# A hybrid encoder layer on one core: w_down's columns taken back and forth, and partial sums put into the banks of the last products

## The chip, the core and the metric

The kernel runs on one core of a Trainium2 chip, and the metric is the device time of one execution in microseconds. TensorE (PE) multiplies matrices and writes to PSUM, eight banks of 128 x 512 fp32; VectorE (DVE) and ScalarE (ACT) read and write both PSUM and the on-chip memory SBUF. Transfers between DRAM and SBUF are asked for on two queues: SyncE's (SP), and GpSimd's (POOL), where a transfer can also add to what stands in DRAM (an accumulating DMA). Both queues are served by the same 16 DMA engines. Each engine and each queue works through its instructions in the order in which they were written; semaphores hold an instruction until what it needs is there.

## What is computed

One layer over 512 tokens of width 2048: RMSNorm, one projection, local attention in one half of the heads and gated linear attention in the other, `w_out`, a residual sum, and then the part that this change touches:

```python
    h = rmsnorm(x, ffn_norm_w[l])
    x = x + (jax.nn.silu(h @ w_gate[l]) * (h @ w_up[l])) @ w_down[l]

return rmsnorm(x, final_norm_w)
```

`w_gate` and `w_up` are 2048 x 5632 and `w_down` is 5632 x 2048. All is fp32. The kernel gets fp32 accuracy from three products of a faster type: every operand is split into a rounded part `hi` and a rest `lo`, and hi*hi, hi*lo and lo*hi are summed in PSUM.

## The kernel before

All engine code is written out by hand in one order. There is no scheduler: each Python call appends one instruction to its engine's queue, and the framework adds the semaphores. SBUF is handed out in slots: `s2` has 70 of 128 x 512, `s4` has 16 of 128 x 1024, `ps` the eight PSUM banks. A slot that was given back goes to the end of its list, and its next user waits until the last one is through.

**`Blocks`** (lines 1119 to 1176) multiplies with weights in 2 x 2 blocks with seven products instead of eight. One step takes one weight block of 512 KB. `load` asks for it on SP, with at most `most` blocks held; `sums` makes four sums on VectorE (L1155 to L1157); `split` makes hi on ScalarE (L1168) and lo on VectorE (L1173). Then `products` issues 42 matmuls of 256 columns. `run` writes for step i: load, split of step i, sums of i+1 and i+2, split of i+1, then the products of step i. So VectorE's list is a step or two ahead of TensorE's.

**`Feed`** is the gate and up projections. Its first five sums are made earlier, during `w_out` (`before_out`, with `most` up to 5, as half-size operations into `s2` slots). `run_urgent` takes one piece of the pending side work each time it is called; at the start that work is the last operands of the feed-forward input (L1033, L1036, ScalarE's L1047).

**`w_down`** has 44 row blocks of 128. Blocks 0 to 3 are multiplied directly in four early jobs, whose results are added to the residual kept in DRAM, `xd`. Blocks 4 to 35, as pairs q = 2 to 17, go through `Down` with the seven products. Blocks 36 to 39 follow in four jobs, one for each block of 512 columns (`later_first`, called the later jobs here), and blocks 40 to 43 in `finish`, token block by token block, with the final norm.

`Down` takes the pairs in three chunks (6, 5 and 5 pairs), and in each chunk the four column blocks c = 0 to 3, and in each of these the chunk's pairs: 64 steps. The operands of a chunk's pairs stay in SBUF over its four columns and are made for the next chunk during the fourth (`make`). Seven PSUM banks hold the seven products of one (chunk, column). At the last pair of each, `evac` copies each bank to SBUF (ScalarE, L1474 and L1476), and a DMA carries it to `md` in DRAM: a plain store on SP in the first chunk (L1481), an accumulating one on POOL afterwards (L1479). Four banks are evacuated at once and three (`late`) before the next step's products.

In the last chunk `ahead` loads, at the second pair of each column, the residual `x1` of the column from `xd` (L1459, four DMAs on SP), and for column 3 the seven sums from `md` as well (L1463). When a column is done, `combine` fetches its seven sums from `md` (L1497, on POOL), makes the four output blocks of them with seven operations (L1503 add, L1504 subtract) and adds them, scaled by `rstd2`, to `x1` (L1517, four operations). It runs piece by piece through `run_urgent`. For column 3 the last banks are added to `m` straight from PSUM (L1469).

The later jobs run through `run_job`: four halves of 12 matmuls of 512 columns (L302 to L304); the stream `st` loads their weights on SP (L183) and splits them (L198 on ScalarE, L199 on VectorE) with a lead of three halves or more; `g_load` and `g_split` (L1299 to L1303) do the same for the gated activations. At a job's end `residual` (L1322) adds each bank, scaled, to `x1`.

Of the kernel before, what the change touches and what calls it, by code (L numbers as in the profile page):

```python
# [117 lines left out]
def layer(nc, tc, x, attn_norm_w, w_in, rel_table, gw_f, gb_f, gw_b, gb_b, gla_norm_w, w_out,  # L118
# [7 lines left out]
    with tc.manual_schedule(), \  # L126
# [124 lines left out]
        class Job:  # L251
            drop = None
            between = None
            tail = None

# [11 lines left out]
        def run_job(j):  # L267
# [4 lines left out]
            banks = [ps.get() for _ in range(4)]  # L272
            per = len(j.kts) // j.n
            for i in range(j.n):
# [9 lines left out]
                for b in range(4):  # L284
                    if j.between:
                        j.between(i, b)
                    for s_, k in enumerate(ks):
# [9 lines left out]
                        else:  # L297
# [4 lines left out]
                            mm(o, xh.t[:, c], wh.t[:, w], start=first, stop=False)  # L302
                            mm(o, xh.t[:, c], wl.t[:, w], start=False, stop=False)  # L303
                            mm(o, xl.t[:, c], wh.t[:, w], start=False, stop=last)  # L304
# [874 lines left out]
        class Feed(Blocks):  # L1179
# [80 lines left out]
            def run(self):  # L1260
                banks = {}
                for i, (u, q) in enumerate(self.seq):
                    if u not in banks:
                        banks[u] = [ps.get() for _ in range(4)]
                    self.most = 3
# [4 lines left out]
                    self.split(i + 1)  # L1270
                    self.products(i, banks[u])
# [4 lines left out]
                    for _ in range(3 if i < 8 else 1):  # L1276
                        run_urgent()
# [76 lines left out]
        class Down(Blocks):  # L1354

            def __init__(self, chunks):
                self.chunks = chunks
                self.begin([(ch, c, q) for ch in range(len(chunks)) for c in range(4) for q in chunks[ch]], 1, 256)  # L1360
                self.x = {}
                self.making = self.operands()
                self.late = []

# [59 lines left out]
            def products(self, i):  # L1424
# [4 lines left out]
                first, last = q == self.chunks[ch][0], q == self.chunks[ch][-1]  # L1429
# [5 lines left out]
                for n, ((wh, wl), x) in enumerate(prods):  # L1435
# [16 lines left out]
                if c == 3:  # L1452
                    put(*self.x.pop(q)["slots"])

            def ahead(self, c):

                x1[c] = [s2.get() for _ in range(4)]
                for t in range(4):
                    sp.dma_start(out=x1[c][t].t, in_=xd[4 * c + t])  # L1459
                if c == 3:  # L1460
                    self.m = [s2.get(F32, [P, 2, 256]) for _ in range(7)]
                    for n in range(7):
                        sp.dma_start(out=self.m[n].t.rearrange("p s c -> p (s c)"), in_=md[7 * c + n])  # L1463

            def evac(self, ch, c, n, bank):

                if ch == len(self.chunks) - 1 and c == 3:
                    m = self.m[n].t.rearrange("p s c -> p (s c)")
# [15 lines left out]
            def evac_late(self):  # L1484
                for e in self.late:
                    self.evac(*e)
                if self.late and self.late[0][0] == len(self.chunks) - 1:
                    urgent.append(self.combine(self.late[0][1]))
                self.late = []

            def combine(self, c):
                if c == 3:
                    m = self.m
                else:
                    m = [s2.get(F32, [P, 2, 256]) for _ in range(7)]
                    for n in range(7):
                        pool.dma_start(out=m[n].t.rearrange("p s c -> p (s c)"), in_=md[7 * c + n])  # L1497
                    for _ in range(4):
                        yield
                M = [None] + [x_.t for x_ in m]  # L1500
                y = [s4.get(F32, [P, 2, 512]) for _ in range(2)]
                lo, up = slice(0, 256), slice(256, 512)
                add = lambda o, x_, y_: dve.tensor_tensor(o, x_, y_, op=OP.add)  # L1503
                sub = lambda o, x_, y_: dve.tensor_tensor(o, x_, y_, op=OP.subtract)  # L1504
                add(y[0].t[:, :, up], M[2], M[1])
                sub(M[3], M[1], M[3])
                yield
                sub(M[5], M[5], M[3])
                add(M[3], M[4], M[3])
                yield  # L1510
                sub(y[0].t[:, :, lo], M[5], M[7])
                add(y[1].t[:, :, up], M[6], M[3])
                yield
                sub(y[1].t[:, :, lo], M[5], M[4])
                put(*m)
                for t in range(4):
                    dve.scalar_tensor_tensor(x1[c][t].t, y[t // 2].t[:, t % 2], rstd2[:, t:t + 1], x1[c][t].t,  # L1517
                                             op0=OP.mult, op1=OP.add)
                    if t % 2:
                        yield  # L1520
                put(*y)

            def run(self):
                for i, (ch, c, q) in enumerate(self.seq):
# [6 lines left out]
                    self.evac_late()  # L1531
# [5 lines left out]
                    if c == 3 or i % 3:  # L1537
                        self.make(1)
                    for _ in range(2 if ch == len(self.chunks) - 1 and i % 2 else 1):
                        run_urgent()  # L1540
                    if ch == len(self.chunks) - 1 and c == 3:
# [179 lines left out]
```

## Time and profile before

| what | value |
|---|---|
| runs shown | 2231.3, 2232.7, 2233.52 us, median 2232.7 |
| the profiled execution | 2230.92 us, of which the profile's span is 2229.0 |
| TensorE matmul busy | 2206.4 us, 99% of the span |
| VectorE, ScalarE, GpSimd busy | 1632.0, 998.5, 108.1 us |
| `Feed` | about 862 to 1753 us |
| `Down`: chunk 0, 1, 2 | from 1796.9, 1917.8, 2018.6 us |
| last column of `Down` ends | about 2123 us |
| later jobs, then `finish` | about 2126 to 2176 us, to the end |

A row of groups in the profile gives the line, the engine, the operation, the tiles written and read (their numbers left out), the shapes and the count, then busy time, mean duration, and the idle time of the engine just before it with what ended it. A row of waits gives: who waited for whom, us in total, times, longest. A row of the table by stage gives, from:to, the length, then for TensorE's matmuls, its weight loads, VectorE, ScalarE and GpSimd the busy us and the count, then the granted clock of TensorE, the share of the 16 DMA engines that were busy (1 is all of them; small errors let it pass 1), and GB/s. In the views of DMA, q1 is SP's queue and q0 POOL's: packets, MB, share of the engines. A matmul is shown longer than the distance to the next one, as matmuls overlap.

### The profile page before, as it was taken

Reading aid. Unit: us, or ns where it says so; the run is one execution under the profiler, and the core shown is the slowest. Engines: PE = TensorE matmul, PEld = TensorE weight load, DVE = VectorE, ACT = ScalarE, POOL = GpSimd, SP = SyncE. Lnnn points to the kernel's source line nnn. Section 1 sums busy time; section 2 is a strip of 40 time slices with the busy share of each in tenths; the row PEclk is TensorE's granted clock in tenths of the full one; section 3 lists DMA queues with packets and bytes.
Section 4 is the critical chain, followed back from the end, with each engine's and each line's share of the span. In section 5 each row is a group of like instructions: output and inputs, shape, how many; then the busy total and the mean of one; then the engine's idle time right before and its main releaser. Section 6 shows DMA issues by size and latency. Waiting matters only on the chain.

```text
span 2229.0 us, 37056 instructions
## 1 busy us (share of the span) xinstructions
PE 2206.4 (99%) x14842; PEld 2039.6 (91%) x14842; DVE 1632.0 (73%) x2748; ACT 998.5 (45%) x1644; POOL 108.1 (5%) x163
## 2 busy tenths in 40 slices
PE   9999999999999999999999999999999999999988
PEld 7888888888888888999999999999999999999967
DVE  4366665644454447988888888888888788887985
ACT  6244454444453345434444344434443565555442
POOL 0000000000000100000000000000000110122300
PEclk9999999999999999999999999999999999999999
DMA  6525625231314432333333333333333865688962
GB/s 206 168 76 155 177 77 140 85 116 55 104 60 148 142 133 67 114 119 119 114 123 118 115 126 115 123 116 114 124 114 114 258 179 190 178 200 224 288 219 76
DMA packets 212201, 305.93 MB, mean 137 GB/s; under 512 B 15229, under 2 KB 133421, under 8 KB 212030
## 3 DMA queue, kind: packets, MB, share of 16 engines
q1 hardware_dynamic: 194366, 258.87, 36.4%
q0 software_dynamic: 17344, 44.18, 8.2%
q8 instruction: 116, 1.90, 0.3%
q10 hardware_dynamic: 320, 0.53, 0.1%
q14 instruction: 55, 0.45, 0.1%
HBM read 246.58 MB, written 44.37 MB: 131 GB/s over the span
## 4 chain that ended last, share of the span: by engine, by line
PE 94%; DVE 3%; DMA 2%; SPq 0%; issue 0%; ACT 0%; POOL 0%; DVEq 0%
PE ps L1216 13%; PE ps L1215 13%; PE ps L1214 13%; PE ps L303 6%; PE ps L304 6%; PE ps L302 6%; PE ps L296 5%; PE ps L294 5%; PE ps L295 5%; PE ps L1443 4%; PE ps L1444 4%; PE ps L1442 4%; PE ps L530 1%; DMA a<-md 1%; PE ps L870 1%; PE ps L539 1%
## 5 line engine op out<-in xcount | busy, mean ns | idle before, releaser
L1216 PE MATMUL ps<-a,b 128*128 128x256 f32 x2464 | 698.9, 284 | 1.8 <-DVE b L1173 1.8
L1214 PE MATMUL ps<-a,b 128*128 128x256 f32 x2464 | 698.9, 284 | 0.0
L1215 PE MATMUL ps<-a,b 128*128 128x256 f32 x2464 | 698.7, 284 | 0.0
L1168 ACT CAST b<-b 128x1024 fp32r<-128x1024 f32 (+1 forms) x475 | 439.9, 941 | 537.6 <-DVE b L1173 311.0
L1173 DVE TENSOR_TENSOR b<-b,b 128x1024 fp32r<-128x1024 f32 (+1 forms) x475 | 503.0, 1087 | 116.5 <-PE ps L1215 60.9
L1216 PEld LDWEIGHTS ps<-a,b 128*128 128x128 f32 x2464 | 474.0, 192 | 2.0 <-DVE b L1173 2.0
L1214 PEld LDWEIGHTS ps<-a,b 128*128 128x128 f32 x2464 | 474.0, 192 | 0.0
L1215 PEld LDWEIGHTS ps<-a,b 128*128 128x128 f32 x2464 | 473.9, 192 | 0.0
L199 DVE TENSOR_TENSOR a<-b,a 128x512 fp32r<-128x512 f32 x292 | 194.7, 686 | 142.5 <-ACT a L198 131.4
L1443 PE MATMUL ps<-b,a 128*128 128x256 f32 x896 | 254.5, 284 | 2.6 <-DVE b L1173 2.6
L1444 PE MATMUL ps<-b,a 128*128 128x256 f32 x896 | 254.1, 284 | 0.0
L1442 PE MATMUL ps<-b,a 128*128 128x256 f32 x896 | 254.0, 284 | 0.0
L198 ACT CAST a<-b 128x512 fp32r<-128x512 f32 x292 | 170.7, 618 | 42.9 <-DMA b<-in_w_in_dram 12.8
L303 PE MATMUL ps<-a,a 128*128 128x512 f32 x464 | 181.7, 392 | 4.6 <-DVE a L199 4.6
L302 PE MATMUL ps<-a,a 128*128 128x512 f32 x464 | 183.2, 395 | 2.8 <-ACT a L198 2.8
L304 PE MATMUL ps<-a,a 128*128 128x512 f32 x464 | 181.1, 390 | 0.0
L1443 PEld LDWEIGHTS ps<-b,a 128*128 128x128 f32 x896 | 172.3, 192 | 3.5 <-DVE b L1173 3.5
L1442 PEld LDWEIGHTS ps<-b,a 128*128 128x128 f32 x896 | 172.4, 192 | 0.0
L1444 PEld LDWEIGHTS ps<-b,a 128*128 128x128 f32 x896 | 172.3, 192 | 0.0
L1155 DVE TENSOR_TENSOR b<-b 128x512 f32<-128x512 f32 x235 | 160.8, 684 | 11.6 <-DMA b<-in_w_down_dram 11.6
L294 PE MATMUL ps<-a,a 128*128 128x512 f32 x416 | 167.0, 401 | 0.4 <-ACT a L198 0.4
L296 PE MATMUL ps<-a,a 128*128 128x512 f32 x416 | 162.9, 392 | 0.2
(243 smaller groups left out, 3072.0 us busy)
## 6 DMA issues: line engine op xcount, KB each, us to landing
b<-in_w_gate_dram SPq DMA_DIRECT2D x88, 512.0 KB, 3.5
b<-in_w_up_dram SPq DMA_DIRECT2D x88, 512.0 KB, 3.8
b<-in_w_down_dram SPq DMA_DIRECT2D x88, 512.0 KB, 6.1
b<-in_w_in_dram SPq DMA_DIRECT2D x48, 512.0 KB, 3.9
b<-in_w_in_dram SPq DMA_DIRECT2D x92, 256.0 KB, 4.2
b<-in_w_out_dram SPq DMA_DIRECT2D x32, 512.0 KB, 5.9
md<-a POOLq DMA_DIRECT2D x49, 256.0 KB, 8.4
a<-a SPq DMA_DIRECT2D x96, 128.0 KB, 2.3
```

The costliest lines, as they stand in the source:

```text
L294: mm(o, wh.t[:, c], xh.t, start=first, stop=False)
L302: mm(o, xh.t[:, c], wh.t[:, w], start=first, stop=False)
L303: mm(o, xh.t[:, c], wl.t[:, w], start=False, stop=False)
L304: mm(o, xl.t[:, c], wh.t[:, w], start=False, stop=last)
L1168: act.copy(o, src)
L1173: dve.tensor_tensor(o, src, h, op=OP.subtract)
L1214: mm(o, wh, xh, start=head, stop=False, skip_group_check=True)
L1215: mm(o, wh, xl, start=False, stop=False, skip_group_check=True)
L1216: mm(o, wl, xh, start=False, stop=end, skip_group_check=True)
L1442: mm(o, xh[:, t], wh, start=first and h == 0, stop=False, skip_group_check=True)
L1443: mm(o, xh[:, t], wl, start=False, stop=False, skip_group_check=True)
L1444: mm(o, xl[:, t], wh, start=False, stop=last, skip_group_check=True)
```

## The change

1. `Down` takes the columns of chunk 1 in the order 3, 2, 1, 0. So chunk 0's column 3 and chunk 1's column 3 follow each other, and the seven banks are not evacuated between; likewise column 0 from chunk 1 to chunk 2.
2. The combining no longer touches `x1`. It writes its result into the `md` tiles in SBUF, two operations a step, from four steps after the fetch. Column 3's `md` tiles are fetched on SP during column 2.
3. `seed` copies the combined blocks into four PSUM banks (ScalarE, eight copies of half a bank), and the later job of that column starts with its matmuls adding to these banks. One `residual` then adds all to `x1`. Column 0's seeds are copied during the last step of `Down`, the other columns' at the third half of the job before.
4. `x1` is loaded only in the later jobs, at the second half of each.
5. The first weights of the later jobs are asked for one step earlier, and a second load is allowed in the step after.
6. In `Feed`, five loads may be held in the first two steps and one more set of sums is made in each of them in the half-size form; `run_urgent` is called twice a step, not three times, in steps 2 to 7.

```diff
-            banks = [ps.get() for _ in range(4)]
+            banks = j.banks or [ps.get() for _ in range(4)]
...
+                            on = bool(j.banks)
+                            mm(o, xh.t[:, c], wh.t[:, w], start=first and not on, stop=False, skip_group_check=on)
...
-                    self.most = 3
+                    self.most = 5 if i < 2 else 3
...
+                    if i < 2:
+                        self.sums(self.n_sums, halves=True)
...
-                    for _ in range(3 if i < 8 else 1):
+                    for _ in range(3 if i < 2 else 2 if i < 8 else 1):
...
+                cols = lambda ch: range(3, -1, -1) if ch % 2 else range(4)
+                self.begin([(ch, c, q) for ch in range(len(chunks)) for c in cols(ch) for q in chunks[ch]], 1, 256)
...
+                third = 0 if ch % 2 else 3
+                first = q == self.chunks[ch][0] and (ch == 0 or c != 3 - third)
+                last = q == self.chunks[ch][-1] and (ch == self.end or c != third)
...
                             self.evac(ch, c, n, self.banks[n])
+                            if ch == self.end and c == 3:
+                                self.seed(0, n)
...
+            def fetch(self, c, ns, queue):
+
+                self.m.setdefault(c, {})
+                for n in ns:
+                    m = self.m[c][n] = s2.get(F32, [P, 2, 256])
+                    queue.dma_start(out=m.t.rearrange("p s c -> p (s c)"), in_=md[7 * c + n])
...
-                if ch:
+                if (c, n) in self.stored:
                     pool.dma_start(out=md[7 * c + n], in_=y.t, accum_op=OP.add)
                 else:
                     sp.dma_start(out=md[7 * c + n], in_=y.t)
+                    self.stored.add((c, n))
...
+            def evac_late(self, i):
+                late, self.late = self.late, []
+                for e in late:
                     self.evac(*e)
+                if late and late[0][0] == self.end:
+                    c = late[0][1]
+                    if c < 3:
+                        self.fetch(c, range(7), pool)
+                        i += 4
                     for n in range(7):
+                        self.ops.append((i, c, n))
+
+            def combine(self, i, n):
+
+                while n and self.ops and self.ops[0][0] <= i:
+                    _, c, k = self.ops.popleft()
+                    n -= 1
+                    m = self.m[c]
...
+                    dve.tensor_tensor(m[o].t, m[x_].t, m[y_].t, op=op)
...
+            def seed(self, c, t):
...
+                for h in range(2):
+                    act.copy(b.t[:, h * 256:(h + 1) * 256], self.y[c][t // 2][h].t[:, t % 2])
...
-                    if ch == len(self.chunks) - 1 and q == self.chunks[ch][1]:
-                        self.ahead(c)
...
+                    if ch == self.end:
                         n = self.chunks[ch].index(q)
+                        self.combine(i, 2)
+                        if c == 2 and n:
+                            self.fetch(3, range(2 * n - 2, min(2 * n, 7)), sp)
+                        if c == 3:
+                            if n == 0:
+                                g_load(LAST // 2 - 2)
+                            if n == 1:
+                                st.until, st.limit = None, 1
+                                st.load()
+                            if n == 2:
+                                g_split(LAST // 2 - 2)
+                                g_load(LAST // 2 - 1)
+                                st.limit = 2
+                                st.load()
...
-                run_urgent()
+                dn.combine(len(dn.seq), 2 if c else 1)
+                if i == 1:
+                    x1[c] = [s2.get() for _ in range(4)]
+                    for t in range(4):
+                        sp.dma_start(out=x1[c][t].t, in_=xd[4 * c + t])
+                if i == 2 and c < 3:
+                    for t in range(4):
+                        dn.seed(c + 1, t)
```

More of the change, by code (lines that the diff above doesn't have):

```diff
@@ L254, in layer @@
             tail = None
+            banks = None
         def job(kind, pieces, kts, acts, evac, rate=0.0, before=None, start=None, limit=None):
@@ L1359, in __init__ @@
                 self.chunks = chunks
-                self.begin([(ch, c, q) for ch in range(len(chunks)) for c in range(4) for q in chunks[ch]], 1, 256)
+                self.end = len(chunks) - 1
+                cols = lambda ch: range(3, -1, -1) if ch % 2 else range(4)
+                self.begin([(ch, c, q) for ch in range(len(chunks)) for c in cols(ch) for q in chunks[ch]], 1, 256)
                 self.x = {}
@@ L1363, in __init__ @@
                 self.late = []
+                self.stored = set()
+                self.m, self.y = {}, {}
+                self.ops = deque()
             def source(self, ch, c, q):
@@ L1451, in products @@
                     put(hi, lo)
-                if c == 3:
+                if c == third:
                     put(*self.x.pop(q)["slots"])
[L1455 to L1463, printed above, removed]
+            def fetch(self, c, ns, queue):
[3 more added lines that the diff above has]
+                    queue.dma_start(out=m.t.rearrange("p s c -> p (s c)"), in_=md[7 * c + n])
             def evac(self, ch, c, n, bank):
-                if ch == len(self.chunks) - 1 and c == 3:
-                    m = self.m[n].t.rearrange("p s c -> p (s c)")
+                if ch == self.end and c == 3:
+                    m = self.m[c][n].t.rearrange("p s c -> p (s c)")
                     dve.tensor_tensor(m, m, bank.t, op=OP.subtract if n == 4 else OP.add)
@@ L1491, in combine @@
[L1491 to L1495, printed above, removed]
-                    for n in range(7):
[L1497 to L1521, printed above, removed]
```

48 lines of the change are left out of this document (23 added, 25 removed).

## The prediction

> **What bounds the kernel now.** I read the busy shares, TensorE's waits, a table by stage, and then, stage by stage, what VectorE and the two DMA queues did before each wait.
>
> ```profile
> PE 2206.4 (99%) x14842; PEld 2039.6 (91%) x14842; DVE 1632.0 (73%) x2748; ACT 998.5 (45%) x1644; POOL 108.1 (5%) x163
> ...
> PE ps L303 <- DVE a L199: 4.6, 6, 1.4
> PE ps L302 <- ACT a L198: 2.8, 1, 2.8
> PE ps L1443 <- DVE b L1173: 2.6, 3, 1.2
> PE ps L1216 <- DVE b L1173: 1.8, 1, 1.8
> ```
>
> TensorE is the bound; the change leaves its number of matmuls as it is, so only its waits can be won. The table by stage shows where they lie:
>
> ```profile
> core 0: us, PE busy (x) PEld busy (x) DVE busy (x) ACT busy (x) POOL busy (x), PEclk, DMA share, GB/s
> 860.00:900.00 40.00, 38.16 (x313) 37.67 (x312) 30.53 (x57) 24.45 (x42) 2.16 (x4) 1.00 0.24 80
> 900.00:1757.00 857.00, 857.00 (x7130) 856.36 (x7128) 748.35 (x1130) 351.97 (x415) 11.18 (x21) 1.00 0.38 122
> ...
> 1797.00:2044.00 247.00, 247.00 (x2061) 247.00 (x2060) 214.44 (x334) 143.41 (x206) 30.72 (x35) 1.00 0.69 193
> 2044.00:2069.00 25.00, 24.83 (x208) 24.63 (x207) 16.71 (x25) 10.32 (x16) 7.47 (x13) 1.00 0.99 284
> 2069.00:2096.00 27.00, 25.76 (x215) 25.56 (x214) 22.91 (x35) 12.82 (x18) 12.00 (x18) 1.00 1.03 280
> 2096.00:2123.00 27.00, 25.77 (x213) 25.36 (x211) 20.90 (x30) 9.64 (x13) 7.17 (x11) 1.00 1.06 311
> 2123.00:2150.00 27.00, 19.61 (x79) 13.90 (x78) 23.91 (x39) 14.06 (x25) 2.14 (x4) 1.00 0.81 296
> 2150.00:2176.00 26.00, 26.00 (x116) 21.54 (x115) 26.00 (x43) 8.50 (x15) 0.00 (x0) 1.00 0.24 82
> ```
>
> The first row holds the start of the feed-forward blocks; the rows 2044, 2069 and 2096 are columns 1, 2 and 3 of the last chunk of `Down` (DMA share at 1); 2123:2150 are the first two `later` jobs (VectorE at 24 of 27). In 900:1757 and 1797:2044 TensorE has no gap, at 0.12 us a matmul (857/7130), so a step of 42 matmuls is 5.04 us. The four waits sum to 11.8 us. As a matmul of 256 columns is shown at 0.284 us but issued each 0.12, and one of 512 at 0.39 but each 0.22 (26/116), a wait costs some 0.17 us more than shown: 11 waits, 13.6 us in all. That is the most this change can win; all else stays.
>
> **Turning the columns.** At the two turns the seven banks are kept. 14 evacuations on ScalarE and 14 of 49 accumulating DMAs go; they stand beside a TensorE that in 1797:2044 waits for nothing. Price 0, no cover needed. (Seven of the others become plain stores on SP, ahead of weight loads that are asked for three steps, 15 us, early.)
>
> **Start of the feed-forward blocks.** `most = 5` and early sums change VectorE's order.
>
> ```profile
> 870.44 0.96 DVE L1173 TENSOR_TENSOR b<-b,b 128x768 fp32r<-128x768 f32 x1 [4.65 <-ACT b L1168]
> ...
> 881.60 2.57 DVE L1033 TENSOR_TENSOR a<-a,a 128x256 f32<-128x256 f32 x5
> 884.09 0.69 DVE L1155 TENSOR_TENSOR b<-b 128x512 f32<-128x512 f32 x1
> ...
> 885.61 0.95 DVE L1173 TENSOR_TENSOR b<-b,b 128x768 fp32r<-128x768 f32 x1
> ```
>
> TensorE waits 1.8 us for the split that starts at 885.61. Ahead of it stand a set of sums (884.09 to 885.61, 1.5 us) and two subtractions at the end of the 881.60 group (1.3 us). The sums go to step 0, into the 4.65 us that VectorE idles before 870.44; of three turns of `run_urgent` one moves behind the split. So it starts 2.8 us earlier, and 1.8 is needed: the wait goes, -2.0 us. What grows: the sums are six half-size operations, some 1.9 us, and the set in step 1 delays the operand work by as much, partly under a ScalarE wait. Bounds: 0 and -2.0; I take -2.0, since the margin is 1 us.
>
> **The last chunk of `Down`.** Here VectorE was late because of DMA and because of the work that is removed.
>
> ```profile
> DVE b L1155 <- DMA b<-in_w_down_dram: 8.1, 2, 4.4
> ...
> 2078.35 0.69 DVE L1155 TENSOR_TENSOR b<-b 128x512 f32<-128x512 f32 x1
> ...
> 2081.88 0.68 DVE L1155 TENSOR_TENSOR b<-b 128x512 f32<-128x512 f32 x1
> ...
> L1517 DVE SCALAR_TENSOR_TENSOR a<-b,small,a 128x512 f32<-128x512 f32 x8 | 5.6, 745 | 0.0
> ...
> L1504 DVE TENSOR_TENSOR b<-a,a 128x512 f32<-128x512 f32 x4 | 2.7, 685 | 0.0
> ```
>
> A step costs VectorE 3.5 us (2078.35 to 2081.88) of 5.04. A column had seven combining operations of 0.67 and four additions to x of 0.70 (L1517) besides: 17.7 + 4.7 + 2.8 = 25.2 of 25.2 us, and nothing was left to make good the 8.1 us of waiting for weights (a load took 11.3 us from issue, below). The four L1517 go (their work is done later by the one `residual` that is there anyway), so 2.8 us a column are spare. The combining starts four steps after its fetch, not two, so its wait for `md` goes too. All 2.6 us of TensorE's waits (3.1 with the 0.17) would go, if the weights came no later. They move as follows:
>
> ```profile
> q0 software_dynamic: 1518, 3.54, 68.2%
> q1 hardware_dynamic: 1273, 2.41, 34.2%
> ...
> b<-in_w_down_dram SPq DMA_DIRECT2D x5, 512.0 KB, 11.3
> ...
> a<-xd SPq DMA_DIRECT2D x4, 256.0 KB, 12.0
> ...
> q1 hardware_dynamic: 1893, 3.90, 104.6%
> ...
> q0 software_dynamic: 489, 0.89, 93.9%
> q1 hardware_dynamic: 96, 0.20, 12.4%
> ```
>
> These are the DMA views of 2069:2091 (first four lines), 2126:2136 (3.90 MB in 10 us: SP's queue alone moves 0.39 MB/us) and 2043:2049. With POOL's accumulations and fetches under way SP's queue gets 2.41/22 = 0.11 MB/us, at worst 0.20/6 = 0.03. Column 1 loses 1.05 MB of x loads: its weights come earlier. Column 2 loses them too, but gets column 3's seven `md` tiles (1.84 MB), two behind each weight load: 5 x 0.52 + 1.84 = 4.5 MB on SP's queue. It can move 2.4 + 3.2 us x 0.39 = 3.7 MB in its 25.2 us. The weights of column 3's fourth step end at 4.2 MB, so 0.5 MB is left for column 3's accumulations: 5 us at 0.11, about 30 us after column 2 began. Sums and split need 2.5 more: 32.5, against seven steps or 35.3 at which TensorE asks for the split that stands behind these sums. The fifth step's 0.8 MB come 7 us later: 39.5 against 40.3. So at the average rate TensorE just does not wait; at the worst, 0.5 MB take 16 us and it waits 9. Bounds 0 (TensorE cannot issue faster than without a gap) and +9; I take +1.6, near the first, since 22 us of row stand against 6.
>
> [...]
>
> **From `Down` to `later`.**
>
> ```profile
> DVE a L199 <- ACT a L198: 8.8, 1, 8.8
> ...
> 2101.75 2.13 SPq L1459 DMA_DIRECT2D a<-xd  x4
> 2103.97 8.41 SPq L1463 DMA_DIRECT2D a<-md  x7
> ...
> 2114.41 8.81 SPq L183 DMA_DIRECT2D b<-in_w_down_dram  x7
> ```
>
> The first weights of `later` were queued on SP behind x and `md`, at 2114; VectorE idled 8.8 us for them and TensorE 2.8. Both groups leave this place, the load is asked for a step earlier, and waits only for a buffer that column 3's first step frees: some 5 us into column 3, about 2098 on the new clock, 20 us before it is used. The wait goes, -2.9 us. If it lands late after all, ScalarE's seeds and casts queue behind it.
>
> **In `later`.**
>
> ```profile
> L199 DVE TENSOR_TENSOR a<-b,a 128x512 fp32r<-128x512 f32 x20 | 13.2, 692 | 8.8 <-ACT a L198 8.8
> ...
> L1517 DVE SCALAR_TENSOR_TENSOR a<-b,small,a 128x512 f32<-128x512 f32 x8 | 5.5, 748 | 0.0
> L1469 DVE TENSOR_TENSOR a<-a,ps 128x512 f32<-128x512 f32 x7 | 4.3, 681 | 0.0
> ...
> 894.94 0.37 ACT L1230 COPY a<-ps 128x256 f32<-128x256 f32 x1 [0.18 <-PE ps L1216]
> ```
>
> TensorE's six waits (4.6 us, 5.6 with the 0.17) are VectorE's lateness. It loses 8 L1517 (5.5 us) and starts up to 8.8 us earlier. What is left per job of 48 matmuls (10.3 us): job 0 three additions of 0.61, four splits of 0.66, a gate split of 1.4, four combinations of 0.67, a residual of 2.8 = 11.5; job 1 nine splits, eight combinations, gate split and residual = 15.5; jobs 2 and 3 about 10 and 8. Job 1 alone exceeds its 10.3, by 5, but its splits run three or more halves (2.6 us each) ahead. I take +0.6 of waits left, bounds 0 and +5.
>
> Seeds: 32 copies of half a bank. The other direction (PSUM to SBUF) is 0.37 us, so 3.0 us a job on a ScalarE that is busy 14 of 27; below it the copy might cost nothing visible, above it 0.6 as for a whole bank. They are emitted two halves (5 us) ahead of their job: 0 on the path. Behind them on ScalarE stand casts, and behind those VectorE's splits. The x loads (16 DMAs, 12.0 us to landing in the full queue, less when it is a quarter full as in 2150:2176) follow weight loads on SP; they are due at the end of their job; a late one would hold VectorE's `residual` and the splits behind it. Price 0, bound by job 0 alone, up to +4.
>
> **Sum.** -2.0 - 3.1 + 1.6 - 2.9 - 5.6 + 0.6 = -11.4 us against the profiled execution's 2230.9 (span 2229.0), that is 2219.5; the median of the runs shown, 2232.7, is 1.8 above that execution, so 2221.3.
>
> **Rivals.**
> 1. The weights come late (column 2's extra 0.8 MB): 4 to 9 us of new waits in column 3. For it: DMA share 1.03 to 1.06. Against: column 1 starts column 2 without the old backlog. 2224 to 2229. Chance 0.17.
> 2. `later` stays VectorE-bound: job 1 waits its 5 us. For: 26.00 of 26 in 2150:2176. Against: 8.8 us of idle time become usable. 2225.7. Chance 0.08.
> 3. The other side: SP's queue is starved at 0.03 MB/us in columns 2 and 3 alike, 9 us of wait each. It decides from 18 us (13.6 won, 4.5 measurable): 2237. For: the 2043:2049 row. Against: that row covers 6 us, the 22 us average is 0.11. Chance 0.07. [...]
> 4. The freed waits come back elsewhere (operand work, x loads): within 0.2%. Chance 0.06.
>
> The forecast, 2217.5 to 2224.5, has 0.62. A measurement can tell about 0.2%, 4.5 us. With rival 1's upper end within that, faster 0.85 (0.15 of rival 1 in it), same 0.07, slower 0.08. The range 2217 to 2228 takes in rival 2 and most of 1.
>
> **What would show it.** Right: no L1216 wait at 884; no PE wait in columns 1 and 2; `later` begins without an L198 wait; L1517 gone and VectorE below 24 in the first two jobs. The DMA step is wrong if L1443 waits in column 3 exceed 3 us, or if none is left. Wrong altogether if PE waits for seeds (ScalarE's new copies), or if `residual` waits for x.

## The result, and the profile after

The changed kernel takes 2216.1 us (median of six runs, 2215.51 to 2216.53) against 2232.5 us (six runs, 2231.3 to 2233.52): a ratio of 0.9926, 95% interval 0.9914 to 0.9939. It is faster, as forecast, but by 16.4 us and not by 11.4; the forecast of 2221.3 and its range of 2217.5 to 2224.5 were too high.

The busy line of the changed kernel's page; VectorE has 8.5 us less in all than before:

```profile
PE 2204.3 (100%) x14842; PEld 2040.1 (92%) x14842; DVE 1623.5 (73%) x2740; ACT 1003.0 (45%) x1664; POOL 96.0 (4%) x149
```

TensorE's waits in the same profile (who waited for whom: us, times, longest), all of them:

```profile
PE ps L907 <- DVE warm L388: 1.1, 1, 1.1
PE ps L346 <- DMA b<-in_x_dram: 0.4, 1, 0.4
```

Both lie in the first 12 us. All 11 waits on which the forecast rests are gone, and none came in their place. The table by stage, in the stretches of the table of before:

```profile
core 0: us, PE busy (x) PEld busy (x) DVE busy (x) ACT busy (x) POOL busy (x), PEclk, DMA share, GB/s
860.00:900.00 40.00, 40.00 (x326) 39.49 (x326) 33.03 (x67) 26.09 (x46) 2.17 (x4) 1.00 0.26 83
...
2044.00:2069.00 25.00, 25.00 (x211) 25.00 (x210) 18.82 (x28) 12.52 (x18) 10.35 (x15) 1.00 1.00 257
2069.00:2096.00 27.00, 27.00 (x228) 27.00 (x227) 20.55 (x31) 13.72 (x19) 11.64 (x17) 1.00 1.05 303
2096.00:2123.00 27.00, 27.00 (x210) 26.23 (x209) 24.42 (x37) 15.74 (x28) 4.91 (x9) 1.00 1.06 340
2123.00:2150.00 27.00, 27.00 (x121) 22.36 (x120) 26.25 (x44) 21.72 (x48) 2.13 (x4) 1.00 0.89 328
2150.00:2176.00 26.00, 26.00 (x116) 21.52 (x116) 15.15 (x28) 5.59 (x14) 0.00 (x0) 1.00 0.19 61
```

TensorE is busy in the whole of every stretch. The DMA engines are as full as before. VectorE does less in 2069:2096 and has caught up by 2150:2176 (15.15 us, where it had 26.00). Yet it waits longer for weights than before, and TensorE doesn't feel it (VectorE's waits, 2040 to 2120 us):

```profile
DVE b L1157 <- DMA b<-in_w_down_dram: 10.4, 6, 3.4
```

Both kernels issue 14842 matmuls. Only chunk 1 of `Down` has its columns in another order, and every step there has 42 matmuls in both. So I matched them by their place in the list and read how much earlier each starts. All below is worked out from these starts in the two profiled executions:

| stretch | forecast | measured |
|---|---|---|
| first 12 us (start-up) | 0 | +1.1 |
| start of the feed-forward blocks | -2.0 | -2.05 |
| last chunk of `Down` | -3.1 + 1.6 | -3.7 |
| boundary and later jobs | -2.9 - 5.6 + 0.6 | -9.7 |

Outside the start-up the change won 15.4 us of profiled time, more than the 13.6 that "is the most this change can win". Two questions follow: which part of the change carried each stretch, and why a removed wait was worth more than its price.

### The profile page after: what moved, and what is told of

It reads as the page before. It is cut to its first block, busy times and chain, and to the rows that moved or that the text cites. A ratio compares the mean times of both kernels' runs of the same rounds, so it can differ in the third digit from the quotient of the medians.

```text
span 2214.8 us, 37040 instructions
## 1 busy us (share of the span) xinstructions
PE 2204.3 (100%) x14842; PEld 2040.1 (92%) x14842; DVE 1623.5 (73%) x2740; ACT 1003.0 (45%) x1664; POOL 96.0 (4%) x149
## 4 chain that ended last, share of the span: by engine, by line
PE 99%; DVE 1%; DMA 0%; SPq 0%; ACT 0%; issue 0%; DVEq 0%
PE ps L1217 13%; PE ps L1216 13%; PE ps L1218 13%; PE ps L304 7%; PE ps L306 7%; PE ps L305 7%; PE ps L297 5%; PE ps L295 5%; PE ps L296 5%; PE ps L1457 5%; PE ps L1456 5%; PE ps L1455 5%; PE ps L532 1%; PE ps L872 1%; PE ps L541 1%; PE ps L540 1%
## 5 line engine op out<-in xcount | busy, mean ns | idle before, releaser
L1456 PE MATMUL ps<-b,a 128*128 128x256 f32 x896 | 253.6, 283 | 0.0
L198 ACT CAST a<-b 128x512 fp32r<-128x512 f32 x292 | 170.8, 618 | 31.9 <-DMA b<-in_w_in_dram 10.9
L1456 PEld LDWEIGHTS ps<-b,a 128*128 128x128 f32 x896 | 172.0, 192 | 0.0
```

The source lines that it names most:

```text
L1456: mm(o, xh[:, t], wl, start=False, stop=False, skip_group_check=True)
```

## The experiments

Except for two more executions of the kernel before, every kernel here is the changed kernel with an edit, and its time stands against 2216.1. Measured beside them, the kernel before had medians of 2232.3 to 2233.5, so these times can be compared. "Margin" is the time from the end of VectorE's split of a step to the first matmul that reads it, from the single instructions of a trace. Steps 44 to 63 are the last chunk, five to a column. The margin is 0.05 to 1.9 us in steps 52 to 56 and 59 to 62 of the kernel before; in the changed kernel it is 4.3 to 6.3 in steps 50 to 56, and least at step 59, 1.2.

### The last chunk: VectorE

```diff
-                        i += 4
+                        i += 2
...
-                    for n in range(7):
+                    for n in range(9 if c < 3 else 7):
...
+                    if k > 6:
+                        for t in (2 * k - 14, 2 * k - 13):
+                            dve.scalar_tensor_tensor(m[0].t, m[2].t, rstd2[:, t:t + 1], m[4].t, op0=OP.mult, op1=OP.add)
```

> The changed kernel with VectorE's part of the last chunk put back: the combining starts two steps after its fetch, not four, and four operations of the size of the old additions to x follow it in columns 1 to 3 (on tiles that are no longer needed, so the output is unchanged). Nothing is put back on SP's queue. In the changed kernel VectorE ends a split 1.2 to 2.0 us before TensorE asks for it in steps 59 to 62 (the first four of column 3), and 3.2 to 6.3 us in the steps before. Theory V (the waits went because VectorE has 2.8 us a column less to do and waits for md no more): these margins are used up, TensorE waits 1 to 4 us in columns 2 and 3, time 2217 to 2220. Theory D (the waits went because x left SP's queue): no wait comes back, 2216 within 1 us.

Measured: 2222.1 us (2221.99 to 2222.29). The waits of this kernel in the last chunk:

```profile
DVE a L1524 <- DMA a<-md: 9.3, 4, 5.7
...
PE ps L1456 <- DVE b L1175: 3.8, 2, 2.4
...
DVE b L1157 <- DMA b<-in_w_down_dram: 3.1, 1, 3.1
```

VectorE's part matters: theory D alone is out. But 3.8 us of waits cost 6.0: after the longer one the granted clock is at half for 3.4 us (0.71, 0.50 and 0.93 in the three stretches of 2 us from 2066 to 2072), which costs 1.5 more (see the price of a wait, below). The combining and the extra operations were separated by two more kernels. First the early combining without the four operations:

```diff
-                        i += 4
+                        i += 2
```

> The changed kernel with the combining two steps after its fetch, without the four extra operations a column. The run with both had 3.8 us of TensorE waits and 9.3 us of VectorE waiting for md. Theory V1 (VectorE's waiting for md is what counts: it stands in VectorE's list ahead of the next splits): a TensorE wait of 1.5 to 2.5 us in column 1 as there, time 2218 to 2221. Theory V2 (the four operations count): no wait in column 1, at most 0.5 us in all, time 2216 to 2217.

Measured: 2222.2 us (2219.9 to 2222.58).

```profile
DVE a L1518 <- DMA a<-md: 14.5, 5, 6.7
...
PE ps L1456 <- DVE b L1175: 4.3, 2, 3.3
```

Then the four operations with the late combining (the rest of the first diff, `i += 4` kept):

> The changed kernel with the four extra VectorE operations of the old size a column (2.8 us), and the combining four steps after its fetch as in the changed kernel. The other half of the run with both. If waiting for md is the whole of VectorE's lateness: no TensorE wait above 0.3 us, 2216 within 1 us. If the 2.8 us a column count by themselves, as the prediction's sum had it (nothing left to make good the late weights): 0.5 to 2.5 us of waits in column 3, where the margin was 1.2 us, 2217 to 2219.

Measured: 2216.5 us (2215.52 to 2217.12), no wait on L1456; the margin at step 59 is 1.55. So V1 holds: the work that was taken from VectorE was worth nothing by itself, with the early combining (2222.1 against 2222.2) or with the late one. What counts is that the fetch of `md` has four steps, 20 us, in which to land. With two, VectorE stands up to 6.7 us at the combining, with the next steps' sums and splits behind it.

### The last chunk: SP's queue

```diff
+                    if ch == self.end and q == self.chunks[ch][1]:
+                        for t in range(4):
+                            d = s2.get()
+                            sp.dma_start(out=d.t, in_=xd[4 * c + t])
+                            put(d)
```

> The changed kernel with the traffic of x put back where it was: at the second step of each column of the last chunk four loads of 256 KB from xd on SP, into spare slots that nobody reads (the real loads stay in the later jobs). VectorE's work is unchanged. 1.05 MB more on SP's queue a column, at 0.11 MB/us 9.5 us later weights in columns 2 and 3, at the 0.39 of a free queue 2.7 us later. Theory D: TensorE waits 3 to 9 us, nearly all in column 3, where the margin is 1.2 us; time 2219 to 2225. Theory V: VectorE's margin holds it, under 1 us, time 2216 to 2217.

Measured: 2220.4 us (2219.52 to 2221.6).

```profile
DVE b L1157 <- DMA b<-in_w_down_dram: 14.1, 4, 7.7
...
PE ps L1456 <- DVE b L1175: 2.2, 1, 2.2
```

So this relief was needed too, against V; but D's place was wrong. The wait is at 2069, at the first step of column 2, and there is none in column 3. x of column 1 stood ahead of those weights on SP, and beside them column 0's accumulations and fetches were under way on POOL until 2068. Why column 3 was spared was not followed up.

> Both of the two together: combining early with the four operations, and the traffic of x on SP's queue. If the two margins add up (either theory alone is half of it), the waits are more than the sum of the two alone, 5 to 12 us, 2221 to 2228; by V as with the early combining alone, by D as with the traffic alone.

Measured: 2223.5 us (2223.25 to 2223.7), TensorE waits 4.9 us in four. The two neither add (3.8 and 2.2) nor does one cover the other: VectorE waits 6.9 us for `md` here and 4.0 for weights, where it waited 14.1 for weights with the traffic alone. The margins are again those of the kernel before, 0.05 to 0.5 us in steps 53 to 63: the two conditions together remake its last chunk.

Now the transfers that the forecast feared, doubled:

```diff
                 for n in ns:
+                    if queue is sp:
+                        d = s2.get(F32, [P, 2, 256])
+                        queue.dma_start(out=d.t.rearrange("p s c -> p (s c)"), in_=md[n])
+                        put(d)
```

> The changed kernel with the seven md tiles that are fetched on SP in column 2 fetched twice (the first into spare slots that nobody reads): 1.84 MB more on SP's queue in column 2. By the prediction's 0.11 MB/us 17 us later weights in column 3; by the rate of the changed kernel's trace there (2.48 MB in 17 us, 0.146 MB/us) 12.6 us; by a free queue's 0.39, 4.7 us. VectorE's margin is 1.2 us. TensorE waits of 3 to 4 us in column 3 by the last, 8 to 16 us by the others; 2219 to 2234. If the tight place is not there: under 2 us, 2218.

Measured, one execution: 2225.6 us; VectorE's and TensorE's waits in the last chunk:

```profile
DVE b L1157 <- DMA b<-in_w_down_dram: 20.5, 8, 6.4
...
PE ps L1456 <- DVE b L1175: 6.6, 2, 5.7
```

The place was right: column 3, steps 59 to 62, has the least margin, and 1.84 MB more cost 6.6 us of wait there. With the 1.2 us of margin that is some 7.8 us for 1.84 MB, 0.24 MB/us: between the free queue's 0.39 and the forecast's 0.11. (Of the rest of the 9.5 us, 1.3 is a stretch of slow clock (mean granted clock of the run 0.997, of the changed kernel 0.999), 0.5 the start after each wait, both below, and 0.5 a later start-up.) What SP's queue got in the changed kernel itself, in 2093:2110 (POOL's q0 first):

```profile
q0 software_dynamic: 1175, 2.41, 67.3%
q1 hardware_dynamic: 1048, 2.48, 40.6%
```

That is 0.146 MB/us, where the forecast took 0.11.

### The turned columns

The columns were put back into the order 0 to 3 in each chunk, and the release of the operands with it:

```diff
-                cols = lambda ch: range(3, -1, -1) if ch % 2 else range(4)
+                cols = lambda ch: range(4)
...
-                first = q == self.chunks[ch][0] and (ch == 0 or c != 3 - third)
-                last = q == self.chunks[ch][-1] and (ch == self.end or c != third)
+                first = q == self.chunks[ch][0]
+                last = q == self.chunks[ch][-1]
```

> The changed kernel with the columns always in the order 0 to 3: 14 more evacuations on ScalarE and 14 more accumulating DMAs, all else kept. The prediction priced the turning at 0: 2216.1 within 1 us, no new TensorE wait. Rival: the accumulations that the turn to column 0 leaves out stood before the weights of the last chunk's first columns (VectorE's margin in steps 42 to 49 is 2 us larger in the changed kernel than before); without the turns a wait of 0.5 to 3 us in the last chunk, 2217 to 2220.

Measured: 2216.95 us (2215.97 to 2217.23), no TensorE wait after the start. Price 0 holds. The turns do buy margin: without them it is 1.3 us at step 52, with them 4.5.

### The start of the feed-forward blocks

```diff
-                    self.most = 5 if i < 2 else 3
+                    self.most = 3
...
-                    if i < 2:
-                        self.sums(self.n_sums, halves=True)
...
-                    for _ in range(3 if i < 2 else 2 if i < 8 else 1):
+                    for _ in range(3 if i < 8 else 1):
```

> The changed kernel with the three edits at the start of the feed-forward blocks undone. The prediction gave them -2.0 us (a wait of 1.8 us plus 0.17 for a lost overlap): 2216.1 + 2.0 = 2218.1, with one TensorE wait of 1.8 us for VectorE's split at about 884 us. If the edits of the last chunk had changed more than their own place, or if the margin of the start is there anyway, 2216 and no such wait.

Measured: 2219.3 us (2218.96 to 2221.2), one wait of 1.8 us at 885, as forecast (which of the three edits takes it away was not separated); but the matmuls behind it start 3.6 us later, not 2.0. The table by stage of this kernel shows the rest:

```profile
884.00:887.50 3.50, 1.65 (x14) 1.45 (x13) 3.43 (x7) 2.91 (x6) 0.00 (x0) 1.00 0.30 88
887.50:891.00 3.50, 3.50 (x23) 3.50 (x23) 3.43 (x7) 0.87 (x2) 0.00 (x0) 0.69 0.19 66
891.00:894.50 3.50, 3.50 (x27) 3.50 (x26) 3.43 (x6) 1.86 (x3) 0.00 (x0) 0.83 0.00 0
```

The granted clock, third from the right, falls to 0.69 and 0.83: 23 and 27 matmuls where 3.5 us hold 31. In the profiled execution of before, the same wait had no such consequence:

```profile
884.00:887.50 3.50, 1.66 (x14) 1.45 (x13) 3.43 (x7) 2.92 (x4) 0.00 (x0) 1.00 0.49 150
887.50:891.00 3.50, 3.50 (x31) 3.50 (x30) 3.43 (x6) 0.87 (x2) 0.00 (x0) 1.00 0.02 5
```

### The price of a wait

To measure it by itself, waits of graded length were made where TensorE otherwise never waits:

```diff
+            def burden(self, i):
+                if i >= 24 and i % 10 == 4 and i < 168:
+                    d = s2.get()
+                    for _ in range(7 + (i - 24) // 10 % 5):
+                        dve.tensor_tensor(d.t, rb[2].t, rb[2].t, op=OP.add)
+                    put(d)
...
                     self.sums(i + 2)
+                    self.burden(i)
                     self.split(i + 1)
```

> The changed kernel with 15 bursts of 7 to 11 idle additions (0.69 us each) on VectorE in the feed-forward blocks, every tenth step, ahead of a split; the output is unchanged. VectorE's margin there is 4.2 us, so TensorE should wait 0.6, 1.3, 2.0, 2.7 and 3.4 us, three times each, 30 us in all. Theory A (a wait costs its idle time and some 0.17 us, as the prediction had it): 2216 + 30 + 15 x 0.17 = 2249, the granted clock at 1.00. Theory B (a wait of 1.8 us or more can halve the clock for some 3.4 us, by chance, as after the waits of 1.8, 2.2 and 2.4 us in the runs so far): one half or so of the nine longer ones cost 1.6 us more, 2253 to 2264. [...]

Measured, one execution: 2261.3 us. Thirteen of the bursts made a wait, of 0.15 to 3.9 us. Two of nearly equal length, 2.27 us before 1362.45 and 2.19 us before 1415.96, and the stretch after each:

```profile
1359.00:1362.50 3.50, 1.23 (x11) 1.02 (x10) 3.40 (x6) 0.00 (x0) 0.00 (x0) 1.00 0.47 146
1362.50:1366.00 3.50, 3.34 (x26) 3.14 (x27) 3.43 (x6) 1.17 (x2) 0.00 (x0) 1.00 0.01 4
1412.50:1416.00 3.50, 1.31 (x12) 1.10 (x10) 3.40 (x6) 0.00 (x0) 0.00 (x0) 1.00 0.46 136
1416.00:1419.50 3.50, 3.50 (x17) 3.31 (x18) 3.43 (x7) 1.78 (x2) 0.00 (x0) 0.57 0.06 19
```

The first left the clock at 1.00, after the second it was 0.57, and 0.94 in the 3.5 us behind that. Seven of the ten waits of 1.5 us or more were followed by such a stretch (mean granted clock of the run 0.992, of the changed kernel 0.999), of some 3.4 us with matmuls each 0.21 us and not 0.12. Besides the idle time and the start after it, the stretch cost 1.5 to 1.6 us each time; after the wait of 3.9 it was longer and cost 2.5. Theory B holds.

Does this touch the kernel before? Two more executions of it:

> The kernel before once more. Its profiled execution (2230.9) showed the clock at 1.00 after each wait and is 1.6 us faster than the median of its runs. If the half clock after a wait of 1.8 us or more comes by chance (it has two such waits, 1.8 and 2.8 us), other executions show it after one of them and are 1.6 us longer, about 2232.5; if not, this one is like the first in every wait, and its time differs in the first 12 us alone.

> As the run ahead of it: the kernel before, one more execution. A slow stretch of 1.5 to 1.7 us after the wait at 884 or at 2123 in one of the two at least, if it comes by chance with a half; none in either, if the waits of the kernel before do not cause it.

Measured: both 2232.8 us, that is 1.8 above the first profiled execution. In one, the clock was at 0.78 and 0.73 after a wait of 3.0 us at the boundary, but at 1.00 after the one at 884. In the other it fell after both. The stretches after the boundary in the one, then after the wait at 884 and after the boundary (3.4 us) in the other:

```profile
2128.00:2131.50 3.50, 3.27 (x10) 2.20 (x11) 3.50 (x7) 3.47 (x6) 0.00 (x0) 0.78 1.05 388
2131.50:2135.00 3.50, 3.50 (x13) 2.73 (x12) 3.50 (x7) 3.50 (x8) 0.00 (x0) 0.73 1.04 394
...
887.50:891.00 3.50, 3.50 (x23) 3.50 (x22) 3.43 (x7) 0.87 (x2) 0.00 (x0) 0.63 0.14 47
...
2128.00:2131.50 3.50, 3.50 (x8) 2.48 (x9) 3.50 (x7) 3.47 (x6) 0.00 (x0) 0.50 1.05 387
2131.50:2135.00 3.50, 3.50 (x11) 2.71 (x10) 3.50 (x7) 3.50 (x8) 0.00 (x0) 0.60 1.04 394
```

So the same program draws differently in each execution, and the execution on which the forecast was built had drawn none. The start-up adds its own part: against that execution, these two are 1.5 and 0.4 us later by their 600th matmul. It had the earliest start-up of all 17 profiled executions here.

Matched matmul by matmul, the two come out at 1.9 us behind it by different ways. In the first, 1.5 us are start-up and 0.4 slightly longer waits in `Down`. Its slow clock at the boundary cost nothing in the end: TensorE was 1.9 us behind ahead of it, 2.1 in it and 1.9 again by 2138, because the wait of 1.0 us for VectorE that the first profiled execution has at 2131 did not come. In the second, 0.4 us are start-up and 1.5 the slow clock after 884; its slow clock at the boundary was made up for in the same way by 2138. So the half clock makes up most of the 1.8 in one of the two. In the other the expected 1.6 us came true in the number by the start-up alone: that was luck.

### The boundary and the later jobs

The first weights asked for in the third step of column 3, as before:

```diff
-                            if n == 1:
-                                st.until, st.limit = None, 1
-                                st.load()
...
-                                st.limit = 2
-                                st.load()
+                                st.until, st.limit = None, 1
+                                st.load()
```

> The changed kernel with the first weights of the later jobs asked for where they were (third step of column 3, one block), some 5 us later than in the changed kernel, but with no x and no md ahead of them on SP. The prediction put the whole wait of 2.9 us to the weights' place in the queue and gave the earlier step no price of its own. If x and md ahead of them were the cause: landing at about 2114, 5 us before the first later job, no wait above 0.3 us, 2216.1 within 1 us. If the step earlier is needed: TensorE waits 1 to 3 us at the start of the later jobs (about 2119), 2217.5 to 2219.5.

Measured: 2215.6 us (2215.41 to 2215.76), no wait. The earlier step isn't needed; what x and `md` leave in the queue is enough. Without the seeds (the calls of `seed` go too, and the first job combines two operations at a time like the others):

```diff
                     residual(c, t, banks[t])
+                for t in range(4):
+                    for h in range(2):
+                        o = x1[c][t].t[:, h * 256:(h + 1) * 256]
+                        dve.scalar_tensor_tensor(o, dn.y[c][t // 2][h].t[:, t % 2], rstd2[:, t:t + 1], o,
+                                                 op0=OP.mult, op1=OP.add)
+                put(*dn.y[c][0], *dn.y[c][1])
```

> The changed kernel without the seeds: the later jobs start their banks themselves, and the combined sums are added to x1 on VectorE after the residual, by eight operations of 128 x 256 a job (about 0.43 us each, 3.4 us a job). In the changed kernel VectorE is busy 39.2 of the 41.3 us of the four later jobs and TensorE waits for nothing. By the prediction's reading (the waits in the later jobs are VectorE's work): 52.8 us of work in 41.3, less a lead of some 5 us: TensorE waits 4 to 9 us, 2220 to 2225. Rival (the waits there came from the late start, the 8.8 us for the first weights): at most 1.5 us, 2216 to 2217.5.

Measured: 2216.9 us (2216.63 to 2217.19), one TensorE wait of 0.7 us. This contradicted the forecast's reading. Where the work went, later jobs and `finish`, without the seeds and in the changed kernel:

```profile
2119.00:2160.00 41.00, 40.27 (x178) 33.03 (x177) 40.93 (x74) 17.13 (x30) 2.13 (x4) 1.00 0.77 280
2160.00:2205.00 45.00, 45.00 (x207) 37.55 (x206) 35.60 (x73) 11.50 (x35) 0.00 (x0) 1.00 0.21 71
```

```profile
2119.00:2160.00 41.00, 41.00 (x182) 33.97 (x181) 38.90 (x64) 27.93 (x61) 2.13 (x4) 1.00 0.81 293
2160.00:2205.00 45.00, 45.00 (x208) 37.59 (x207) 26.58 (x53) 11.94 (x36) 0.00 (x0) 1.00 0.21 70
```

VectorE is full, but 9 us of its work slide into `finish`, where it has time. So the late start remained as the cause; it was put back with the old traffic ahead of the weights (with the edit of the weights above):

```diff
+                    if ch == self.end and c == 3 and q == self.chunks[ch][1]:
+                        for n in range(11):
+                            d = s2.get(F32, [P, 2, 256])
+                            sp.dma_start(out=d.t.rearrange("p s c -> p (s c)"), in_=md[n])
+                            put(d)
```

> The changed kernel with the first weights of the later jobs asked for where they were (third step of column 3, one block) and, ahead of them on SP at the second step of column 3, eleven loads of 256 KB from md into spare slots that nobody reads: the traffic of x and md that stood there before. Seeds and VectorE's work stay as changed. Theory L (the late start made the waits at the boundary and, through VectorE's missing lead, those in the later jobs): TensorE waits 2 to 3 us at the boundary and 1 to 4 us in the later jobs; 2219 to 2224. Theory W (VectorE's additions made those in the later jobs): 2 to 3 us at the boundary, under 0.5 us after it; 2218.5 to 2220. If the queue's order is not the cause of the boundary's wait either: 2216.

Measured: 2224.6 us (2223.26 to 2225.61).

```profile
DVE a L199 <- ACT a L198: 12.3, 1, 12.3
...
PE ps L304 <- ACT ps L1530: 5.3, 1, 5.3
```

At the boundary TensorE waits 5.3 us, not 2 to 3, and for a seed (L1530): ScalarE copies the seeds behind the casts that wait for the late weights. Then the clock is slow for some 5 us (down to 0.50), 2.5 us more. The wait is longer than the 2.8 us of the kernel before because TensorE is 4.7 us earlier at the boundary (2118.6 against 2123.3), but the first cast of the weights (L198) only 2.8 earlier (2122.5 against 2125.3); the copies of the seeds come on top. In the later jobs nothing: not theory L's 1 to 4 us. With both undone:

> The late start and the seeds undone together (the additions after the residual, eight of 128 x 256 a job). Without the seeds alone 0.7 us of wait (1.0 of time) came back. If late start and additions work through one lead of VectorE's: more than the two alone together, boundary 2 to 3 us and 5 to 9 us in the later jobs, 2223 to 2229. If they are independent: the late start alone plus 1 us.

Measured: 2227.6 us (2226.97 to 2228.61).

```profile
PE ps L304 <- ACT a L198: 5.3, 1, 5.3
...
PE ps L305 <- DVE a L199: 2.7, 1, 2.7
```

TensorE waits as long at the boundary, so the seeds only change the name of what is waited for. In the later jobs 2.7 us of wait appear and some 1.4 lost to slow clock (mean granted clock of the run 0.996, with the late start alone 0.997), against 0 (late start alone) and 1.0 (additions alone). So late start and additions draw on one lead of VectorE; either alone nearly leaves it whole, as the changed kernel's 38.9 of 41 us suggests. (With the late start TensorE loses 8 us at the boundary itself, in which VectorE can catch up.) The six short waits of the kernel before (1.4 us at most) were not reproduced one by one.

## Why the prediction was right and wrong

- **The sign and the places** were right: each wait that it named went, and no rival came. No TensorE wait is for a seed, and `residual` waits for no x.
- **Turning the columns, price 0**: right.
- **Start of the feed-forward blocks, -2.0**: right, by place and size (2.05).
- **Last chunk, +1.6 of new waits for weights**: this step failed; no such wait came. The forecast's own sum at 0.11 MB/us already ended without a wait, by 0.8 us (39.5 against 40.3); the 1.6 was leaned towards the worst row, 0.03 MB/us over 6 us. The weights did come late (10.4 us of VectorE's waits), and column 3 is the tight place, but SP's queue got 0.146 MB/us and 1.2 us of margin were left. The rate of 0.11 came from 22 us of the kernel before, in which POOL's queue moved 3.54 MB; in 2093:2110 of the changed kernel SP's moves 2.48 MB against POOL's 2.41. In 2068:2074 it is 0.17 against 0.81 (last section).
- **Last chunk, what frees VectorE**: three reliefs were named, and only two carry: the four steps for `md`, and x gone from the queue. The four L1517, on which the sum of "25.2 of 25.2 us" rests, are worth 0 by themselves.
- **Boundary, -2.9**: right, and by the queue's order as argued. The step earlier adds nothing. Unforeseen was that a late boundary would now cost 5.3 us and a slow clock.
- **Later jobs, -5.6 + 0.6**: the -5.6 came; the +0.6 of job 1 did not. Work per job was counted as if it were due in its job; without the seeds 9 us of it moved to `finish` and TensorE lost 1.0.
- **"13.6 us in all"**: undersized. Besides the idle time shown and the 0.17 us, the matmul after the released one starts some 0.10 us late (0.12 with 512 columns), 11 times: 1.2 us.
- **"the median ... is 1.8 above that execution"**: this step failed too. The 1.8 was carried over whole to a kernel that has lost the waits. In the two further executions of the kernel before, it was start-up (1.5 and 0.4), longer waits (0.4 in one) and clock lost after the wait at 884 (1.5 in the other). A start-up later than that of the profiled execution came with the changed kernel too (1.1 us); the rest goes with the waits. The profiled time less the 15.4 us won is 2215.5, and the changed kernel's median is 0.6 above that, not 1.8.

The miss of 5.2 us is then 4.0 in the sum and 1.2 in the offset. The 4.0 (15.4 us won, 11.4 forecast) are 2.2 of waits that didn't come (1.6 and 0.6), 1.2 for the matmul behind each wait, and 0.6 of remainders that no run explains.

## What to carry to other kernels

Price a wait from start to start of the matmuls (here 0.17 us and some 0.10 more than the idle time shown), and look in the trace for a slow clock behind it (here after some waits from 1.84 us up, 1.3 to 2.5 us each); a single profiled execution shows one draw, so an offset between it and the median may belong to its start-up or to the waits that the change removes. Where an engine's list holds an operation that waits for a fetch, moving that operation later can be worth more than taking work away from it (here 6 us against 0). Before work is called due, look at who needs it: work that only a later stage reads can slide there (here 9 us).

## What the runs showed of the hardware

Behind some of TensorE's waits its granted clock was at half, behind others of the same length at 1.00. TensorE's waits, shortest first, and the granted clock in the stretches of 2 to 6 us behind each:

| run, place in us | wait, us | granted clock behind it |
|---|---|---|
| early combining with the four operations, 2116:2119 | 1.4 | 1.00 |
| before, 884 | 1.84 | 1.00 |
| before, second execution, 884 | 1.84 | 1.00 |
| before, third execution, 884 | 1.84 | 0.63, 0.88 |
| start of the feed-forward blocks undone, 884 | 1.85 | 0.69, 0.83 |
| both conditions in the last chunk, 2116:2121 | 2.0 | 1.00 |
| graded waits, 1414 | 2.19 | 0.57, 0.94 |
| x in SP's queue, 2069 | 2.2 | 0.53, 0.62 |
| graded waits, 1360 | 2.27 | 1.00 |
| early combining with the four operations, 2060:2066 | 2.4 | 0.71, 0.50, 0.93 |
| before, boundary | 2.8 | 1.00 |
| before, second execution, boundary | 3.0 | 0.78, 0.73 |
| before, third execution, boundary | 3.4 | 0.50, 0.60 |
| late start, boundary | 5.3 | 0.50, 0.50, 0.74 |
| late start without seeds, boundary | 5.3 | 0.67 |

A slow stretch lasted about 3.4 us, an estimate from the mean clocks around it that takes 0.50 for all of it; behind the wait of 3.4 us and both of 5.3 about 6.8, a part of which lay in the wait itself. It cost 1.3 to 1.6 us, up to 2.5 after the longest waits, and nothing where TensorE would have waited for VectorE behind it. The wait of 1.84 us is at the same instruction of the same program in all three executions: the clock fell behind it in one. What decides this was not shown.

SP's share of the DMA engines was not the same in two stretches in which POOL's queue was busy too: 40.6% in 2093:2110, 12.5% in 2068:2074. Here are the queues of the changed kernel in 2068:2074, while the seven accumulating transfers of a column, asked for from 2064.9 to 2070.3, were under way on POOL, and weights asked for at 2068.2 on SP:

```profile
q0 software_dynamic: 450, 0.81, 91.4%
q1 hardware_dynamic: 84, 0.17, 12.5%
```

POOL's queue takes 0.81 of 0.99 MB, against 2.41 of 4.94 in 2093:2110, quoted above, and 450 packets to SP's 84. Why the split differs between the two stretches stays open. POOL's queue also moved few bytes for its time there: 0.135 MB/us at 91.4% of the engines, where SP's queue alone moved 0.39 MB/us at 104.6% (2126:2136 of the kernel before).
